# Hybrid attention and SSM encoder block: all gate products ahead of the last SSM output, the forget gate behind it, and z's work pinned behind the SSM's outputs

## The chip, the cores and the metric

The kernel runs on one core of a Trainium2 chip. The metric is the time of one execution on the device in microseconds (us), the median of several runs. TensorE is written PE, VectorE DVE, ScalarE ACT, GpSimd POOL and SyncE SP, as the profile does; PEld is PE's loading of stationary operands.

## The reference

One layer (`DEPTH = 1`) over 16 meta tokens and 1024 frames (L = 1040 positions), width 1024, all in float32:

```python
h = concatenate([meta, x])
xn = rmsnorm(h, norm_mix_g)
q, k, v, f_logit, u, gates = split(xn @ w_in)          # 512, 512, 512, 8, 512, 2048 columns
cum_f = cumsum(log_sigmoid(f_logit + b_forget))
y_a = softmax(q.k/8 + cum_f[t] - cum_f[s], s <= t) @ v @ w_attn_out    # 8 heads of 64
z = gelu(s5(u))                                        # diagonal complex SSM, 32 groups of 16 channels
zg = z @ w_glu
y_s = zg[:, :1024] * sigmoid(zg[:, 1024:])
g = sigmoid(gates)
h = h + (g[:, :1024] * y_a + g[:, 1024:] * y_s) @ w_o
xn = rmsnorm(h, norm_ffn_g)
hid = causal_conv3(xn @ w_up)                          # 5632 columns, val and gate
h = h + (silu(gate) * val) @ w_down
out = rmsnorm(h, norm_final_g)[16:]
```

## The kernel before

Features lie on partitions and positions along the free axis: the normed input is kept as `xhi` and `xlo`, its rounded part and the rest, for all L positions. A float32 product is made as three products of rounded parts (`dense_steps`, L170 to L172: high by high, high by low, low by high), eight slices of 128 input features each, so one block of outputs takes 24 products.

The stages of the part that matters here stand in this order in the program:

1. `u` is projected and written to DRAM. `ssm` (L1522) then works in four quarters of eight groups. For each quarter, `ssm_in` and `ssm_out` make tables, and `ssm_chain` is a generator of three parts: inputs (matmuls, copies on ACT), the scan over chunks of 8 positions (rotations on DVE by `TT`, which records each instruction in `log`; two scans, L1831 and L1832; the states `St`), and the outputs: 16 pairs of small products into PSUM (L1851, L1853), copies on ACT to `Y` (L1854), a GELU activation on ACT (L1855), and a store of `Y` to `y_d` in DRAM, issued by POOL (L1856).
2. `stage_gates` is a generator over the second eight gate chunks (chunk 8 to 15, the SSM branch's gates). Each chunk has 72 products in three blocks, so there are 576. A block ends with a sigmoid on ACT (L500) and a store issued by POOL (L501). `advance(q)` runs this generator up to `BEHIND[q]` products, so gate products fill PE while the SSM's other engines work.
3. `forget` (L522) makes the forget gate's logits in three blocks of 16 products (L526, L527), adds the halves (ACT L528, DVE L529), and forms the log sigmoid and its cumulative sum: DVE, ACT's Exp and Ln (L532, L533), DVE's scan, POOL's scaling (L536), a store to `f_d`. The attention reads `f_d` at 354 us.
4. `load_z` (L611) reads `y_d` back as four tiles `zt` with 32 small DMAs, issued by SP and, for the last quarter, half of them by POOL (L618). `split_z` makes z's high copy on ACT (L623) and the rest on DVE. The GLU's products are seven instead of eight (`seven`, a Strassen form), so sums and differences of z's quadrants are made: for each k of two, DVE L636, POOL L637, DVE L638 and L639, then a copy on ACT (L643) and a subtraction on DVE for each of four forms. k = 0 needs quarters 0 and 2 of the SSM, k = 1 quarters 1 and 3.
5. `project_qk(0, qk)` (L574): queries, then keys, of the first pair of heads, 72 products each in blocks of 272, 384 and 384 positions. Their weights come by `wchunk` with `act=True`: POOL issues the load, ACT casts to the high part (L154) and writes the negated copy (L143), and POOL issues a DMA that adds the weights to it in memory, which gives the low part (L144).
6. `glu` for eight chunks: weight forms (POOL L663, ACT L657, DVE or POOL L137), then `seven` (L232 to L234), then `gate`.

Weight tiles `raw`, `whi` and `wlo` have two buffers each, taken in turn by gate chunk 14, gate chunk 15, the queries, the keys, and then by the GLU's weight forms. The PSUM banks of the gate, forget, query and key blocks are three of tag `mm` and one of tag `po`, the latter taken by every fourth block.

What each engine does first is decided when the program is built: a planner lays the instructions out on a simulated time line, by program order and by when their inputs are ready there, and each engine then takes its own in the order that comes out. `after(a, b)` sets an edge without a semaphore: instruction `a` comes behind `b` in the order of their engine. DMAs issued by an engine stand in that engine's order too.

Of the kernel before, what the change touches and what calls it, by code (L numbers as in the profile page):

```python
# [13 lines left out]
AF = mybir.ActivationFunctionType  # L14
ALU = mybir.AluOpType
# [43 lines left out]
def block_kernel(ctx, tc, x, meta, xbt, x0t, g1t, w_q, w_k, w_v, w_f, w_u, w_g, b_f, w_ao, lam_d, bw_d, cw_d,  # L59
                 d_sk, l_dt, w_glu, w_o, g2, w_up, cwt_d, w_dn, gf, out, dbg=None, upto=99):  # L60
# [4 lines left out]
    V, S, GP, PE, SY = nc.vector, nc.scalar, nc.gpsimd, nc.tensor, nc.sync  # L65
# [34 lines left out]
    ident = cp.tile([P, P], F, name="ident")  # L100
# [7 lines left out]
    u_d = dp.tile([SW // P, P, P // GC, NCH], F, name="u_d")  # L108
# [27 lines left out]
    def split_lo(eng, out_, src, hi):  # L136
        return eng.tensor_tensor(out_, src, hi.bitcast(F), ALU.subtract)  # L137
# [39 lines left out]
    def run(gen):  # L177
        for _ in gen:
            pass
# [124 lines left out]
    g1T = n1.tile([P, KD], F, name="g1T")  # L304
    S.dma_start(g1T, g1t)
    GP.dma_start(xm, meta)
    ssm_log, ssm_loads, ssm_steps = ssm(tc, after, sp, sio, st_ps, ident, u_d, y_d, lam_d, bw_d, cw_d, d_sk, l_dt)
    queue = []

    def load(dst, src):  # L310
# [199 lines left out]
        for i in range(KD, 2 * KD):  # L510
            yield from gate_chunk(i, gp_, False)

    BEHIND = (288, 360, 480, 540, 552)
    gates = stage_gates()
    n_gate = [0]

    def advance(q):
        while n_gate[0] < BEHIND[q]:
            next(gates)
            n_gate[0] += 1  # L520

    def forget():  # L522
        for t, n in BLK:
            ps = mm_ps()
            for i in range(KD):
                PE.matmul(ps[:64, :n], wf[:, i, :], xhi[:, i, t:t + n], start=(i == 0), stop=False)  # L526
                PE.matmul(ps[:64, :n], wf[:, i, :], xlo[:, i, t:t + n], start=False, stop=(i == KD - 1))  # L527
            S.copy(fx[:, t:t + n], ps[32:32 + H, :n])  # L528
            V.scalar_tensor_tensor(out=fl_[:, t:t + n], in0=ps[:H, :n], scalar=bf, in1=fx[:, t:t + n],  # L529
                                   op0=ALU.add, op1=ALU.add)  # L530
        V.scalar_tensor_tensor(out=fx, in0=fl_, scalar=-1.0, in1=fl_, op0=ALU.mult, op1=ALU.max)
        S.activation(fx, fx, AF.Exp, scale=-1.0)  # L532
        S.activation(fx, fx, AF.Ln, bias=one[:H])  # L533
        V.scalar_tensor_tensor(out=fx, in0=fl_, scalar=0.0, in1=fx, op0=ALU.min, op1=ALU.subtract)
        V.tensor_tensor_scan(fl_, one[:H].broadcast_to([H, L]), fx, 0.0, ALU.mult, ALU.add)
        GP.tensor_scalar(fx, fl_, -8.0, 0.0, ALU.mult, ALU.add)  # L536
        GP.dma_start(f_d, fx)
        if "f_d" in dbg:
            SY.dma_start(dbg["f_d"], fx)
# [8 lines left out]
    for q in range(4):  # L548
# [6 lines left out]
            begin(q + 2)  # L555
        if q == 1:
            next(ssm_steps)
    advance(4)
    fl_ = sio.tile([P, L], F, tag="sy", name="fl_", bufs=3)[:H]
    fx = sx.tile([P, 1152], F, tag="Gm", name="fx", bufs=1)[:H, :L]  # L560
    forget()
    st_x.close()
    run(gates)
    st_g.close()
    st_s.close()

# [32 lines left out]
    TH = L // 2  # L599
# [11 lines left out]
    def load_z():  # L611
        zts = []
        for m in range(4):
            tag = "gl" if m % 2 else "ms"
            zt = gz[tag].tile([P, CH, NCH], F, tag=tag, name="zt", bufs=2)
            ym = y_d[m].rearrange("(j c) g n -> g c j n", c=GC)
            for g in range(GQ):
                (GP if m == 3 and g % 2 else SY).dma_start(zt[GC * g:GC * g + GC], ym[g])  # L618
            zts.append(zt)
        def split_z(m):  # L620
            w_ = NC2 if m < 2 else NCH
            zh, zl = (fold(t_[:, m % 2, :CH * w_]) for t_ in zs[m // 2])
            S.copy(zh, zts[m][:, :, :w_])  # L623
            split_lo(V, zl, zts[m][:, :, :w_], zh)

        split_z(0)
        split_z(1)

        def part(r, h_, k):
            return zts[2 * r + k][:, :, NC2 * h_:NC2 * h_ + NC2]  # L630

        T4 = zblock(0, 1)
        for k in range(2):
            fa, fb = (gz["cg"].tile([P, L], F, tag="cg", name="zf", bufs=2) for _ in range(2))
            f1, f2, f3, f4 = (fold(f_[:, TH * q:TH * q + TH]) for f_ in (fa, fb) for q in range(2))
            V.tensor_tensor(f1, part(0, 1, k), part(0, 0, k), ALU.subtract)  # L636
            GP.tensor_tensor(f3, part(1, 1, k), part(0, 1, k), ALU.subtract)  # L637
            V.tensor_tensor(f2, part(1, 1, k), f1, ALU.subtract)  # L638
            V.tensor_tensor(f4, part(1, 0, k), f2, ALU.subtract)  # L639
            for f_, t_ in zip((fa, fa, fb, fb), (T1, T2, T3, T4)):  # L640
                q = 0 if t_ is T1 or t_ is T3 else TH
                hi, lo = t_[0][:, k], t_[1][:, k]
                S.copy(hi, f_[:, q:q + TH])  # L643
                split_lo(V, lo, f_[:, q:q + TH], hi)
            split_z(2 + k)
        return T4
# [875 lines left out]
def ssm(tc, after, sp, sio, s_ps, ident, u_d, y_d, lam_d, bw_d, cw_d, d_sk, l_dt):  # L1522
# [1 line left out]
    V, S, GP, PE, SY = nc.vector, nc.scalar, nc.gpsimd, nc.tensor, nc.sync  # L1524
    n_small = [0]

    log = []

    def TS(*a):
        log.append(V.tensor_scalar(*a))  # L1530
# [31 lines left out]
    def rest():  # L1562
# [71 lines left out]
        m = sm(W)  # L1634
# [166 lines left out]
        def chain(qt):  # L1801
# [44 lines left out]
            for q in range(0, GQ, 3):  # L1846
# [5 lines left out]
                              start=True, stop=False)  # L1852
                    PE.matmul(yo, Tm[:, q + i, :], U[:, q + i, :], start=False, stop=True)  # L1853
                S.copy(Y[:, q:q + nq].rearrange("p a n -> p (a n)"), yps[:, :NCH * nq])  # L1854
            S.activation(Y, Y, AF.Gelu_apprx_tanh)  # L1855
            GP.dma_start(y_d[qt], Y)  # L1856

        yield input_tables, output_tables, chain
        rot.append(rotation(1))
        yield  # L1860

    return log, loads, rest()


_OUTS = [((1, SEQ, D), "float32")]
# [55 lines left out]
```

## Time and profile before

| | us |
|---|---|
| median of 3 runs (lowest, highest) | 1466.59 (1466.46, 1469.03) |
| the profiled execution | 1469.97 |
| its span | 1467.7 |

| engine | busy us | share of the span |
|---|---|---|
| PE | 1430.3 | 97% |
| PEld | 1350.7 | 92% |
| DVE | 1074.6 | 73% |
| POOL | 760.7 | 52% |
| ACT | 723.1 | 49% |

How to read the lines shown below. A line of a timeline has the start in us from the beginning of the span, the duration in us, the engine, the line of the kernel, the operation, its output and inputs by the program's names, the count (x2 where two neighbours were merged), and in square brackets the engine's idle time just before and what ended it. A line of the waits has who waited for whom, the total in us, the times, and the longest. A line of the stretches has the window, its length, the busy time and the number of instructions of PE, PEld, DVE, ACT and POOL, the granted clock of PE (1.00 is full), the busy share of the DMA engines and what they moved in GB/s. L137 is a helper, the subtraction that leaves the low part; the tile's name says which one it is. PE's matmuls overlap, so the spacing of their starts, not their duration, is what one costs.

### The profile page before, as it was taken

The numbers are of one execution on the slowest core, as the hardware profiler recorded it, in microseconds if no ns is written. First come the engines' busy times: TensorE is split into PE (matmuls) and PEld (weight loads), VectorE is DVE, ScalarE is ACT, GpSimd is POOL, SyncE is SP. The second block draws the span as 40 slices with busy tenths as digits, with TensorE's granted clock in tenths as the row PEclk, the third lists the DMA queues.
The fourth block names the chain that finished last, engine by engine and source line by source line (L and its number), as shares of the span: only waits on it lengthen the run. The fifth ranks groups of instructions, "written<-read, shape, count | busy, mean of one in ns | idle before, by whom it ended". The sixth has DMA issues, their size and how long they took to land. (4 is left out here: it accounts for less than half of the span.)

```text
span 1467.7 us, 26536 instructions
## 1 busy us (share of the span) xinstructions
PE 1430.3 (97%) x9646; PEld 1350.7 (92%) x9646; DVE 1074.6 (73%) x2198; ACT 723.1 (49%) x1419; POOL 760.7 (52%) x888
## 2 busy tenths in 40 slices
PE   8999979999999999999999999999999999998997
PEld 8999979988999999999879999999999999776886
DVE  7999868852657676646469977788887667688685
ACT  7646575522646565542646444444444435652433
POOL 1542137740555556515861335555554327889766
PEclk9999989999999999999999999999999999999999
DMA  8676634440126432156963245667753214866413
GB/s 281 177 185 161 151 80 127 149 142 30 37 90 171 137 68 79 44 207 237 268 152 136 81 123 163 170 171 186 181 137 109 87 66 151 308 202 164 144 36 115
DMA packets 89653, 209.31 MB, mean 143 GB/s; under 512 B 14442, under 2 KB 22266, under 8 KB 89140
## 3 DMA queue, kind: packets, MB, share of 16 engines
q1 hardware_dynamic: 70068, 162.55, 33.6%
q0 software_dynamic: 17728, 41.41, 14.7%
q10 hardware_dynamic: 1728, 3.68, 0.7%
q8 instruction: 76, 1.25, 0.4%
q14 instruction: 53, 0.43, 0.1%
HBM read 168.52 MB, written 69.35 MB: 162 GB/s over the span
## 5 line engine op out<-in xcount | busy, mean ns | idle before, releaser
L172 PE MATMUL mm<-xhi,wlo 128*128 128x342 f32 (+2 forms) x488 | 159.4, 327 | 7.4 <-DMA wlo<-in_w_k_dram 7.4
L170 PE MATMUL mm<-xhi,whi 128*128 128x342 f32 (+2 forms) x488 | 160.1, 328 | 1.3 <-DVE q L137 1.0
L171 PE MATMUL mm<-xlo,whi 128*128 128x342 f32 (+2 forms) x488 | 158.6, 325 | 0.0
L1156 POOL TENSOR_TENSOR ov<-ov,og 128x1024 f32<-128x1024 f32 x21 | 51.1, 2434 | 122.7 <-ACT og L1155 118.8
L137 DVE TENSOR_TENSOR sw<-sf,sw 128x512 fp32r<-128x512 f32 x72 | 67.0, 930 | 49.1 <-ACT sw L1147 49.1
L172 PEld LDWEIGHTS mm<-xhi,wlo 128*128 128x128 f32 x488 | 92.9, 190 | 8.0 <-DMA wlo<-in_w_k_dram 7.6
L1147 ACT CAST sw<-sf 128x512 fp32r<-128x512 f32 x72 | 44.9, 624 | 108.6 <-POOL sf L1273 66.6
L170 PEld LDWEIGHTS mm<-xhi,whi 128*128 128x128 f32 x488 | 93.0, 191 | 2.4 <-PE sp L791 0.8
L171 PEld LDWEIGHTS mm<-xlo,whi 128*128 128x128 f32 x488 | 92.9, 190 | 0.4 <-issue 0.2
L840 ACT CAST th<-tp 128x256 fp32r<-128x256 f32 (+3 forms) x120 | 56.1, 472 | 61.4 <-PE tp L833 29.1
L1273 POOL TENSOR_TENSOR sf<-raw,sf 128x512 f32<-128x512 f32 x36 | 61.2, 1699 | 44.4 <-DVE sw L137 43.3
L137 DVE TENSOR_TENSOR tl<-tp,th 128x256 fp32r<-128x256 f32 (+3 forms) x120 | 65.1, 547 | 25.4 <-ACT th L840 24.0
L1273 POOL TENSOR_TENSOR sf<-raw 128x512 f32<-128x512 f32 x36 | 47.5, 1320 | 68.6 <-DMA raw<-in_w_up_dram 35.1
L234 PE MATMUL mm<-xhi,sw 128*128 128x258 f32 (+1 forms) x288 | 81.0, 281 | 0.0
L232 PE MATMUL mm<-xhi,sw 128*128 128x258 f32 (+1 forms) x288 | 80.8, 281 | 0.0
L233 PE MATMUL mm<-xlo,sw 128*128 128x258 f32 (+1 forms) x288 | 80.7, 280 | 0.0
L805 POOL TENSOR_SCALAR pt<-pt,nm 128x144 f32<-128x144 f32 (+4 forms) x72 | 52.2, 738 | 51.7 <-DVE nm L804 50.7
L1325 DVE SCALAR_TENSOR_TENSOR ov<-hv,cwt,ov 128x1024 f32<-128x1024 f32 x36 | 71.2, 1977 | 0.1
L1147 ACT CAST sw<-raw 128x512 fp32r<-128x512 f32 x70 | 43.1, 621 | 54.8 <-PE sp L234 26.2
L803 ACT ACTIVATE pt<-pt,nm 128x144 f32<-128x144 f32 (+4 forms) x72 | 52.9, 736 | 26.8 <-DVE nm L802 26.3
L796 DVE CUSTOM_DVE_ANT_0 pt<-sp,fb 128x328 f32<-128x328 f32 (+8 forms) x112 | 46.4, 429 | 20.1 <-PE sp L791 11.5
L137 DVE TENSOR_TENSOR sw<-raw,sw 128x512 fp32r<-128x512 f32 x70 | 54.7, 784 | 5.4 <-ACT sw L1147 4.9
(719 smaller groups left out, 5715.7 us busy)
## 6 DMA issues: line engine op xcount, KB each, us to landing
raw<-in_w_up_dram SPq DMA_DIRECT2D x44, 512.0 KB, 3.7
t_d<-in_w_dn_dram POOLq DMA_DIRECT2D x44, 256.0 KB, 6.9
ar<-a_d SPq DMA_DIRECT2D x44, 256.0 KB, 5.6
wr<-t_d SPq DMA_DIRECT2D x44, 256.0 KB, 2.8
a_d<-ov SPq DMA_DIRECT2D x21, 512.0 KB, 2.6
wr<-in_w_dn_dram SPq DMA_DIRECT2D x33, 256.0 KB, 4.2
t_d<-in_w_dn_dram SPq DMA_DIRECT2D x22, 256.0 KB, 4.5
t_d<-t_d SPq DMA_DIRECT2D x22, 256.0 KB, 4.5
```

What stands on the lines that cost most here:

```text
L137: return eng.tensor_tensor(out_, src, hi.bitcast(F), ALU.subtract)
L170: yield PE.matmul(ps, whi[:, i, :], ahi[:, i], start=(i == 0), stop=False)
L171: yield PE.matmul(ps, whi[:, i, :], alo[:, i], start=False, stop=False)
L172: yield PE.matmul(ps, wlo[:, i, :], ahi[:, i], start=False, stop=(i == k - 1))
L232: PE.matmul(ps, a[0][:, i], bh, start=(i == 0 and not joins), stop=False, skip_group_check=True)
L233: PE.matmul(ps, a[0][:, i], bl, start=False, stop=False, skip_group_check=True)
L234: PE.matmul(ps, a[1][:, i], bh, start=False, stop=(i == kh - 1), skip_group_check=True)
L803: S.activation(pt[:n, :kc], pt[:n, :kc], AF.Exp, bias=nm[:n, 1:2], scale=0.125, accum_out=nm[:n, 2:3])
L840: S.copy(th[:kn, z:tw], tp[:kn, z:tw])
L1147: S.copy(hi, src)
L1273: sums.append(GP.tensor_tensor(f_, a, b, op))
L1325: V.scalar_tensor_tensor(out=o, in0=h_[:, j:SEQ + j], scalar=cwc(j, m), in1=o, op0=ALU.mult, op1=ALU.add)
```

## The change

- `ssm` also returns `outs`, which holds for each quarter the GELU activation (`outs[0]`, `[2]`, `[4]`, `[6]`) and the issue of its store (`outs[1]`, `[3]`, `[5]`, `[7]`).
- `BEHIND` becomes (288, 360, 480, 576): all gate products are called for ahead of the outputs of quarter 3. `run(gates)`, which finishes the generator, stands ahead of `forget()` and no longer behind it, and `advance(4)` goes.
- z's copies on ACT (L623) are set behind the activation of quarter 2, `outs[4]`; the copies of the forms (L643) behind that of quarter 3, `outs[6]`.
- z's subtractions on DVE in `split_z` and the form at L636 are set behind the last SSM instruction of DVE, `ssm_log[-1]`; POOL's form at L637 behind the issue of quarter 3's store, `outs[7]`.

```diff
-    BEHIND = (288, 360, 480, 540, 552)
+    BEHIND = (288, 360, 480, 576)
...
-    advance(4)
     fl_ = sio.tile([P, L], F, tag="sy", name="fl_", bufs=3)[:H]
     fx = sx.tile([P, 1152], F, tag="Gm", name="fx", bufs=1)[:H, :L]
+    run(gates)
     forget()
     st_x.close()
-    run(gates)
...
-            S.copy(zh, zts[m][:, :, :w_])
-            split_lo(V, zl, zts[m][:, :, :w_], zh)
+            after(S.copy(zh, zts[m][:, :, :w_]), ssm_outs[4])
+            after(split_lo(V, zl, zts[m][:, :, :w_], zh), ssm_log[-1])
...
-            V.tensor_tensor(f1, part(0, 1, k), part(0, 0, k), ALU.subtract)
-            GP.tensor_tensor(f3, part(1, 1, k), part(0, 1, k), ALU.subtract)
+            after(V.tensor_tensor(f1, part(0, 1, k), part(0, 0, k), ALU.subtract), ssm_log[-1])
+            after(GP.tensor_tensor(f3, part(1, 1, k), part(0, 1, k), ALU.subtract), ssm_outs[7])
...
-                S.copy(hi, f_[:, q:q + TH])
+                after(S.copy(hi, f_[:, q:q + TH]), ssm_outs[6])
...
-            S.activation(Y, Y, AF.Gelu_apprx_tanh)
-            GP.dma_start(y_d[qt], Y)
+            outs.append(S.activation(Y, Y, AF.Gelu_apprx_tanh))
+            outs.append(GP.dma_start(y_d[qt], Y))
```

More of the change, by code (lines that the diff above doesn't have):

```diff
@@ L306, in block_kernel @@
     GP.dma_start(xm, meta)
[L307 removed]
+    ssm_log, ssm_outs, ssm_loads, ssm_steps = ssm(tc, after, sp, sio, st_ps, ident, u_d, y_d, lam_d, bw_d, cw_d, d_sk, l_dt)
     queue = []
@@ L1860, in rest @@
         yield
-    return log, loads, rest()
+    return log, outs, loads, rest()
 _OUTS = [((1, SEQ, D), "float32")]
```

2 lines of the change are left out of this document (1 added, 1 removed).

## The prediction

> **What bounds the kernel now**
>
> I read the head of the page first, then PE's list of waits, then the timelines of the engines around the end of the SSM.
>
> ```profile
> span 1467.7 us, 26536 instructions
> PE 1430.3 (97%) x9646; PEld 1350.7 (92%) x9646; DVE 1074.6 (73%) x2198; ACT 723.1 (49%) x1419; POOL 760.7 (52%) x888
> PE mm L172 <- DMA wlo<-in_w_k_dram: 7.4, 1, 7.4
> PE tp L1851 <- DVE St L1533: 1.7, 1, 1.7
> PE mm L170 <- DVE fl__2308 L529: 0.3, 1, 0.3
> ```
>
> TensorE is the bound: 37.4 us of the span are not PE work. The change adds no product and removes none, so it can only move PE's waits. The three waits shown all lie between the SSM's last outputs and the GLU, where the change is; the longest single wait of the whole list is the first, for the low part of the key weights. PE's timeline around them:
>
> ```profile
> 164.94 0.38 PE L1851 MATMUL sp<-St,Gm 128*128 128x130 f32 x2
> ...
> 168.43 0.41 PE L170 MATMUL mm<-xhi,whi 128*128 128x342 f32 x1
> ...
> 174.18 0.29 PE L526 MATMUL po<-xhi,wf 128*64 128x272 f32 x1
> ...
> 178.57 0.46 PE L1851 MATMUL tp<-St,Gm 128*128 128x130 f32 x2 [1.72 <-DVE St L1533]
> ...
> 182.37 0.42 PE L527 MATMUL mm<-xlo,wf 128*64 128x384 f32 x1
> ...
> 187.48 0.32 PE L170 MATMUL mm<-xhi,whi 128*128 128x342 f32 x1
> ...
> 191.22 0.29 PE L170 MATMUL po<-xhi,whi 128*128 128x272 f32 x1
> ...
> 203.18 0.29 PE L170 MATMUL mm<-xhi,whi 128*128 128x272 f32 x1
> ...
> 211.00 0.59 PE L172 MATMUL mm<-xhi,wlo 128*128 128x272 f32 x1 [7.41 <-DMA wlo<-in_w_k_dram]
> 211.39 0.43 PE L170 MATMUL mm<-xhi,whi 128*128 128x272 f32 x1
> ...
> 216.15 0.44 PE L170 MATMUL po<-xhi,whi 128*128 128x384 f32 x1
> ...
> 224.73 0.28 PE L232 MATMUL mm<-zh,ops 128*128 128x260 f32 x1
> ```
>
> In order: outputs of SSM quarter 2 (164.94 to 168.43); 36 products of gate chunk 15 (to 174.18); 19 of the forget gate's 48; a wait for the last states; outputs of quarter 3 (178.57 to 182.37); the other 29 forget products; the last 24 products of gate chunk 15 (187.48 to 191.22); queries; keys, which stop within their first three products for 7.4 us; GLU at 224.73. After the stop the products are slow: 21 of them in 211.39 to 216.15, 0.227 us each. The 24 of the query block from 191.22 have the same shape and end at about 194.2, 0.125 us each. The stretches show why:
>
> ```profile
> 203.20:211.40 8.20, 0.79 (x5) 0.57 (x4) 7.21 (x7) 4.58 (x8) 6.02 (x3) 0.68 0.56 108
> 211.40:216.20 4.80, 4.80 (x23) 4.80 (x23) 4.74 (x5) 4.54 (x5) 2.69 (x4) 0.50 0.30 97
> 174.90:224.70 49.80, 40.38 (x244) 38.31 (x243) 33.94 (x40) 32.84 (x49) 16.90 (x17) 0.90 0.41 103
> ```
>
> (Columns: stretch, length, busy PE, PEld, DVE, ACT, POOL, granted clock, DMA share, GB/s.) The granted clock is 0.50 in the 4.8 us behind the stop. So the stop costs its 7.4 us and then 21 x 0.102 = 2.1 us.
>
> Why were the key weights late? ScalarE and POOL:
>
> ```profile
> 168.10 1.27 ACT L623 CAST zh<-zt 128x520 fp32r<-128x520 f32 x1 [2.63 <-DMA zt<-y_d]
> ...
> 186.43 0.63 ACT L643 CAST z2h<-zf 128x520 fp32r<-128x520 f32 x1 [5.30 <-DVE zf L638]
> ...
> 192.42 1.07 ACT L1855 ACTIVATE Y<-Y 128x1040 f32<-128x1040 f32 x1
> ...
> 198.76 1.04 ACT L154 CAST whi<-raw 128x1024 fp32r<-128x1024 f32 x1
> 199.82 1.28 ACT L500 ACT_TABLE_LOAD   x1
> ...
> 203.95 1.04 ACT L143 ACTIVATE wlo<-whi 128x1024 fp32r<-128x1024 f32 x1
> 205.29 0.92 POOL L144 DMA_DIRECT2D wlo<-in_w_k_dram  x1 [2.85 <-ACT wlo L143]
> 197.07 2.14 POOL L618 DMA_DIRECT2D zt<-y_d  x4 [2.73 <-DMA y_d<-Y]
> ```
>
> The cast of the key weights needs the second buffer of the weight tiles; gate chunk 15 holds it until its last product, at 191.2, because 24 of its products stand behind the forget gate. ScalarE then reaches the cast at 198.76, and cast, negated copy and adding DMA bring the low part at 211.0: 12.2 us from the start of the cast. ScalarE also shows z's copies standing ahead of the SSM's own: one waits 2.63 us at 168.10, just when quarter 2's outputs are done, another 5.30 us up to 186.43, though quarter 3's were done at 182.4, and the last activation comes only at 192.42.
>
> **The change part by part**
>
> *All 576 gate products ahead of the last outputs.* 60 gate products now follow quarter 2's outputs, at (174.18 - 168.43) / 36 = 0.160 us: PE comes to quarter 3's outputs at 168.43 + 9.6 = 178.0. No product is added. The last block's sigmoid and its store on POOL come forward with it; its table load at 199.82, which now parts the key weights' cast from its copy, should go.
>
> *z's DVE work behind the last state.* DVE's rows:
>
> ```profile
> 166.23 1.23 DVE L1831 TENSOR_TENSOR_SCAN wr<-dt,ta 128x520 f32<-128x520 f32 x1
> 168.11 1.22 DVE L636 TENSOR_TENSOR zf<-zt 128x520 f32<-128x520 f32 x1 [0.65 <-DMA zt<-y_d]
> ...
> 170.53 1.27 DVE L1832 TENSOR_TENSOR_SCAN ta<-dt,wi 128x520 f32<-128x520 f32 x1
> ...
> 176.60 1.10 DVE L137 TENSOR_TENSOR zl<-zt,zh 128x520 fp32r<-128x520 f32 x1 [0.98 <-ACT zh L623]
> 177.74 1.42 DVE L1533 TENSOR_TENSOR St<-ta,wr 64x516 f32<-64x516 f32 x2
> ```
>
> The scan at 170.53 could follow the one that ends at 167.46: 3.1 us won; the z split at 176.60, with its wait, holds the last states another 2.0. The states then end at about 179.2 - 5.1 = 174.1. PE comes at 178.0, so its 1.72 us wait goes, under cover of 3.9 us of gate products. Quarter 3's outputs took 3.80 us behind the wait and quarter 2's 3.49: 0.3 us more.
>
> *Forget gate behind the outputs.* Its 48 products cost the same there. Its results are read first at the attention, far off, but its three PSUM banks are taken again by the last two query blocks and the first key block, and copies on ScalarE and adds on DVE must clear them. Today this costs the 0.3 us of the third wait; I take 0 to 0.3 and count 0.3 as won.
>
> *The key weights.* Chunk 15 ends at 178.0, 13.2 us earlier. In the new order the keys begin at 203.18 - 1.72 - 0.3 - 0.3 = 200.9, so the cast must start by about 201.1 - 12.2 = 188.9. It has 10.9 us for that, and ScalarE, which waits for PE's outputs from 178 to 181.5 anyway, has nothing of z to do until their activation, as the pins forbid it. I take no wait: 7.4 + 2.1 us won.
>
> *z's ScalarE and POOL work behind the last activation and its store.* Quarter 3's outputs end at 178.0 + 3.5 = 181.5; a table load like the one at 199.82 (1.28) and the activation (1.07) bring 183.9, and I take 184.3 with the last copy ahead of them, against 193.5. Its store, SP's last z loads and POOL's four follow 9.2 us earlier with it; SP's loads for quarter 2 start some 1.3 us earlier, the length of the copy at 168.10. POOL's difference form for k = 0, below, ran at 185.16 when its data had come, so the pin to the store's issue at 184.3 costs nothing.
>
> *The sum.* 1.72 + 0.3 + 0.3 + 7.4 + 2.1 = 11.8 us; the GLU could begin at 212.9. What may then be late is z and the GLU's weight forms. DVE had 33.9 us of work from 174.9 to 224.7; less 1.4 for the last states and plus the form at 168.11 and one split like that at 176.60, both moved in (2.3), it is 34.8, to be done in 174.1 to 212.9, 38.8 us, of which some 5 are idle while quarter 2's z still loads (4.77 now, first row below). That is some 1 us too much, though splits of the keys' low parts in it are not needed by then. ScalarE has 32.8 less a 1.28 load in the same stretch. I bound the new wait ahead of the GLU by 0 (it fits) and 3 us (DVE's overrun and one misplaced wait, such as the 2.63 above, partly beside each other), and take the middle, 1.5, being near neither.
>
> So 11.8 - 1.5 = 10.3 us. The profiled execution took 1469.97 us, its span 1467.7 and 2.3 around it; it becomes 1459.7. The median of the unprofiled runs is 1466.59, 3.4 lower: 1456.3. Behind the GLU PE stays the bound, so the gain lasts to the end.
>
> **The rivals**
>
> *The hand-over to the GLU binds (gain 3 to 8).* z's work that used to fill DVE's and ScalarE's gaps from 168 to 182 is packed behind the outputs, with forget's chain and the query copies. For it: these rows, two-input DVE operations beside POOL's z form.
>
> ```profile
> 185.13 1.21 DVE L638 TENSOR_TENSOR zf<-zt,zf 128x520 f32<-128x520 f32 x1 [4.77 <-DMA zt<-y_d]
> 185.16 2.35 POOL L637 TENSOR_TENSOR zf<-zt 128x520 f32<-128x520 f32 x1 [5.45 <-DMA zt<-y_d]
> 186.37 2.23 DVE L639 TENSOR_TENSOR zf<-zt,zf 128x520 f32<-128x520 f32 x1
> 209.59 1.17 DVE L639 TENSOR_TENSOR zf<-zt,zf 128x520 f32<-128x520 f32 x1
> ```
>
> The same form takes 2.23 us while POOL's form runs (to 187.5) and 1.17 without it. Packed tighter, both forms and four splits so lengthened add some 6 x 1.06 = 6.4 us to a DVE that has none to spare: 11.8 - 6.4 = 5.4 us gain, 1461.2. Against it: POOL is busy 16.9 of 49.8 us there, so not all coincide. [...] The same loss comes if forget's bank copies stand behind a z copy that waits. If the 6.4 us fall in one piece, the 2.1 us of slow products come on top, as behind the 7.4, and the gain is 3.3: 1463.3; behind 1.72 us only 0.3 came. [...]
>
> *The stop stays (no change).* The planner may leave the cast near 198.76; the keys' low part then lands at 211.0 whatever comes before: 1466.6. For it: z's copies rank ahead of the projection in program order. Against: ScalarE is free when the buffer falls free.
>
> *Slower: the cast falls behind z's last copies.* The rows for it (the first is the z loads' own):
>
> ```profile
> DMA to landing us min/median/max: 2.2/3.6/7.3
> 207.58 1.06 DVE L638 TENSOR_TENSOR zf<-zt,zf 128x520 f32<-128x520 f32 x1
> 215.57 0.64 ACT L643 CAST zh<-zf 128x520 fp32r<-128x520 f32 x1
> ```
>
> POOL's last z load is issued by 199.2 now, 9.2 us earlier then, and lands 3.6 us later: 193.6. The work on k = 1 takes 207.6 to 216.2, 8.6 us: 202.2. A cast there brings the low part at 214.4, 3.4 us after today's: 1470.0. It decides from any cast later than 198.8. For it: ScalarE takes its instructions in one order, and 186.43 shows a copy placed ahead of work that was ready. Against: the buffer is free 16 us before z's last data.
>
> **How the numbers follow**
>
> Forecast (gain 8 to 12.5) 0.66; hand-over 0.14; stop stays 0.07; slower 0.13. The measurement can tell 0.2%, 2.9 us. Faster by more than that: 0.66 + 0.14 = 0.80; within: 0.07; slower: 0.13. The likeliest gives 1456.3. The range leaves out the last two cases: from 11.8 and a little for run spread (1454.0) to the hand-over's worst, in one piece, with as little for spread (1463.6).
>
> **What would show it**
>
> PE's list without the key-weight wait and without the wait for the last states; granted clock 1.00 from 200 to 220; chunk 15's last product near 178, the key cast before 189, the last activation of the SSM near 183 to 185, the first GLU product at 213 to 215. A wait at the GLU's first products for DVE means the first rival; a wait at the first L172 of the keys the second or third. It is wrong altogether if the order elsewhere changes, seen as new PE waits behind 320.

## The result and the profile after

| | before | after |
|---|---|---|
| median of 20 runs each | 1468.24 us | 1464.02 us |
| lowest, highest | 1466.05, 1469.84 | 1461.39, 1469.32 |
| ratio, 95% interval | | 0.9975 [0.9967, 0.9983] |

The change gains some 3.7 us (0.25%, the ratio on 1468.24); 10.3 were predicted. The forecast was a median of 1456.3 us, in a range of 1454.0 to 1463.6. The measured one lies 7.7 us above the forecast, and 1.65 of these are the level of the kernel before: 1468.24 here, 1466.59 when the forecast was made. The page's head:

```profile
span 1466.9 us, 26536 instructions
PE 1430.5 (98%) x9646; PEld 1351.0 (92%) x9646; DVE 1078.1 (73%) x2198; ACT 722.5 (49%) x1418; POOL 760.8 (52%) x888
```

The profiled execution after took 1469.32, the highest of its runs; 2.4 us of that lie in a wait at the very end of the kernel (`tp L1441 <- DVE hs L1451`, 5.1 us here, 2.7 before and in most of the profiles below), far from the change. Lines behind L563 have one less than before. PE's list of waits, the lines that are new or have grown (the second was 1.0 us in two before):

```profile
PE mm L232 <- ACT k L590: 3.5, 1, 3.5
PE mm L170 <- DVE q L137: 3.0, 3, 2.0
PE mm L232 <- DVE kl L137: 1.1, 1, 1.1
```

The key weights' 7.4, the states' 1.7 and the forget bank's 0.3 are gone. In their place stand three waits at the hand-over from the projection to the GLU, in PE's timeline:

```profile
209.03 0.41 PE L170 MATMUL mm<-xhi,whi 128*128 128x384 f32 x1 [1.98 <-DVE q L137]
...
217.00 0.36 PE L232 MATMUL mm<-zh,ops 128*128 128x260 f32 x1 [3.54 <-ACT k L590]
...
219.05 0.56 PE L232 MATMUL mm<-zh,ops 128*128 128x260 f32 x1 [1.08 <-DVE kl L137]
```

1.98 + 3.54 + 1.08 = 6.6 us. The GLU starts at 217.00 instead of 224.73, 7.7 earlier; its last products on `zh` show only 3.6 of it (one row of PE's products on `zh`, before and then after; the last number is the start of the last of them):

```profile
L234 PE MATMUL sp<-zh,ops x32: 277/284/286, 234.4 to 304.5; 128*128 128x260 f32 x32
```

```profile
L234 PE MATMUL sp<-zh,ops x32: 278/282/286, 230.7 to 300.9; 128*128 128x260 f32 x32
```

So some 4 us are lost inside the GLU: the wait of 1.08, and slow products behind the waits, as the stretches show (granted clock in the third column from the right):

```profile
210.00:220.00 10.00, 5.38 (x30) 4.91 (x29) 8.83 (x13) 9.03 (x17) 2.25 (x4) 0.91 0.19 57
220.00:230.00 10.00, 10.00 (x67) 10.00 (x66) 6.22 (x15) 6.76 (x18) 6.47 (x10) 0.75 0.19 58
```

Which queue was late? The engines in order of time, ScalarE, VectorE, then POOL:

```profile
177.52 1.05 ACT L154 CAST whi<-raw 128x1024 fp32r<-128x1024 f32 x1
...
181.50 1.05 ACT L143 ACTIVATE wlo<-whi 128x1024 fp32r<-128x1024 f32 x1
...
184.90 1.08 ACT L1854 ACTIVATE Y<-Y 128x1040 f32<-128x1040 f32 x1
...
208.70 4.43 ACT L622 CAST zh<-zt 128x1040 fp32r<-128x1040 f32 x2 [5.54 <-POOL fx L536]
```

```profile
184.76 1.32 DVE L637 TENSOR_TENSOR zf<-zt,zf 128x520 f32<-128x520 f32 x1 [6.94 <-DMA raw<-in_w_glu_dram]
...
197.88 1.30 DVE L637 TENSOR_TENSOR zf<-zt,zf 128x520 f32<-128x520 f32 x1 [3.00 <-DMA zt<-y_d]
...
202.47 1.23 DVE L534 SCALAR_TENSOR_TENSOR fx<-fl__2336,fx 8x1040 f32<-8x1040 f32 x1
...
204.85 2.31 DVE L535 TENSOR_TENSOR_SCAN fl__2336<-one,fx 8x1040 f32<-8x1040 f32 x1
...
207.76 1.12 DVE L137 TENSOR_TENSOR q<-mm,q 64x384 fp32r<-64x384 f32 x2
210.98 4.39 DVE L137 TENSOR_TENSOR zl<-zt,zh 128x1040 fp32r<-128x1040 f32 x2 [2.09 <-ACT zh L622]
...
218.01 0.89 DVE L137 TENSOR_TENSOR kl<-mm,k 64x272 fp32r<-64x272 f32 x2
```

```profile
182.85 0.91 POOL L144 DMA_DIRECT2D wlo<-in_w_k_dram  x1 [0.41 <-ACT wlo L143]
...
207.33 1.34 POOL L536 TENSOR_SCALAR fx<-fl__2336 8x1040 f32<-8x1040 f32 x1 [6.94 <-DVE fl__2336 L535]
```

The key weights are cast at 177.52 and their low part is asked for at 182.85: that part came as predicted. VectorE stands still twice for z's loads, 6.94 us for quarter 2's (the profile names a weight's DMA there, but the form L637 reads z) and 3.00 us for the last quarter's. Then the forget gate's chain (Exp, Ln, L534, the scan, POOL's scaling) is spread over the hand-over. ScalarE stands 5.54 us still ahead of z's second pair of copies, since that pair's memory is where the forget gate's sum `fl_` lay and POOL reads it until 208.7 (`fl_u` below shows it). VectorE's split of the second query block, which frees a bank for PE, stands behind L534 and the scan. The key copies stand behind z's copies.

### The profile page after: what moved, and what is told of

Its sections match the earlier page's. It is cut to its first block, busy times and chain, and to the rows that moved or that the text cites. A ratio compares the mean times of both kernels' runs of the same rounds, so it can differ in the third digit from the quotient of the medians.

```text
span 1466.9 us, 26536 instructions
## 1 busy us (share of the span) xinstructions
PE 1430.5 (98%) x9646; PEld 1351.0 (92%) x9646; DVE 1078.1 (73%) x2198; ACT 722.5 (49%) x1418; POOL 760.8 (52%) x888
## 5 line engine op out<-in xcount | busy, mean ns | idle before, releaser
L170 PE MATMUL mm<-xhi,whi 128*128 128x342 f32 (+2 forms) x480 | 156.6, 326 | 3.0 <-DVE q L137 3.0
L172 PE MATMUL mm<-xhi,wlo 128*128 128x342 f32 (+2 forms) x480 | 155.5, 325 | 0.0
L171 PE MATMUL mm<-xlo,whi 128*128 128x342 f32 (+2 forms) x480 | 155.0, 323 | 0.0
```

The source lines that it names most:

```text
L170: yield PE.matmul(ps, whi[:, i, :], ahi[:, i], start=(i == 0), stop=False)
L171: yield PE.matmul(ps, whi[:, i, :], alo[:, i], start=False, stop=False)
L172: yield PE.matmul(ps, wlo[:, i, :], ahi[:, i], start=False, stop=(i == k - 1))
```

## The experiments

Three theories of what holds PE at the hand-over were tested one after the other. A: the memory of the forget gate's sum, for which z's copies wait. C: the place of the forget gate's chain in the three engines' orders, whatever its work. B: the amount of work there, VectorE's above all, whatever its order.

Each kernel was timed in five rounds against the kernel before on the same chip. All start from the change, but for `b_fl_u`. The median of the kernel before was between 1466.98 and 1470.00 us in the several rounds, so a difference of 0.1% between two rows says little.

| run | what differs from the change | ratio to before [95%] |
|---|---|---|
| p_gates | without z's pins | 0.9985 [0.9976, 0.9994] |
| p_pins | z's pins alone | 1.0002 [0.9993, 1.0010] |
| fl_u | forget's sum in memory of its own | 0.9959 [0.9945, 0.9972] |
| fl_gm | the same in another slot; queues reordered | 1.0004 [0.9993, 1.0014] |
| b_fl_u | before, with fl_u's edit | 1.0000 [0.9991, 1.0010] |
| f_mid | forget between the last gate product and the outputs | 0.9951 [0.9937, 0.9965] |
| f_early | forget ahead of the last 96 gate products | 0.9964 [0.9948, 0.9980] |
| nochain | without forget's L531 to L535 | 0.9928 [0.9914, 0.9942] |
| tailpin | fl_u; L534 and the scan behind the second query split | 0.9969 [0.9956, 0.9982] |
| nozl_u | fl_u without z's two long remainders | 0.9945 [0.9928, 0.9963] |
| nozl_mid | f_mid without them | 0.9949 [0.9932, 0.9967] |
| bare | without L531 to L535 and without them | 0.9906 [0.9888, 0.9924] |
| f_mid_z | f_mid, the two behind T's forms | 0.9967 [0.9955, 0.9980] |
| f_mid_k0 | f_mid, the two behind the first key split | 0.9974 [0.9963, 0.9984] |
| f_mid_k1 | f_mid, the two behind the second key split | 0.9973 [0.9961, 0.9985] |
| f_pin | f_mid, Exp behind the last activation | 0.9959 [0.9944, 0.9973] |
| f_pin_u | f_pin with fl_u's edit | 0.9963 [0.9951, 0.9976] |
| f_pin_zv | f_pin, the two behind the first six weight remainders | 0.9964 [0.9949, 0.9978] |

**The two halves.** `p_gates` has the change without the lines on z; `p_pins` the lines on z alone.

> Only the gate and forget part of the change, without the pins on z. Theory A: the stop at the key weights goes (9.5 us), z's copies stand ahead of the SSM's outputs again, the wait for fl_ stays but comes behind all query copies, so it costs less than in the changed kernel: ratio 0.993 to 0.996. Theory B (the pins' packing is what costs): the whole gain of 11 us, ratio 0.992 or lower, with VectorE's waits gone.

> Only the pins on z, with the gate and forget order of before. Both theories: the states come some 5 us earlier and PE's 1.7 us wait for them goes, the stop at the key weights stays unless the ScalarE reaches the cast earlier. Theory A: ratio 0.997 to 0.999. Theory B: the packing costs here too, ratio 1.000 to 1.003.

```profile
PE mm L172 <- DMA wlo<-in_w_k_dram: 8.5, 1, 8.5
```

Alone, the pins win the states' wait and leave the 8.5 us stop: nothing, as theory B said and not A. Alone, the gates win the stop but the last activation stays at 189.50, and the gain is 0.15%: less than either theory said. PE's list there has 7.4 us of waits in five places, 3.0 and 2.0 of them for a key and a query split, so the hand-over costs without the pins too. Both together give 0.25%; the intervals of the gates alone and of both overlap.

**The memory.** `fl_u` changes the slot, and no engine's order:

```diff
-    fl_ = sio.tile([P, L], F, tag="sy", name="fl_", bufs=3)[:H]
+    fl_ = sio.tile([P, L], F, tag="U", name="fl_", bufs=2)[:H]
```

`fl_gm` takes `sp.tile([P, 1152], F, tag="Gm", name="fl_", bufs=2)` instead, and `b_fl_u` is the first edit in the kernel before.

> The changed kernel with the forget gate's sums (fl_) in the U slot of the SSM's pool, which z's second pair of tiles does not cover; every engine's order is that of the changed kernel. Theory A (z's copy of quarter 2 on ScalarE waits until POOL has read fl_, because it writes the same memory, and the query and key copies stand behind it): that wait of 5.5 us goes, with it PE's 1.98 + 3.54 + 1.08 us and the slow products behind them, about 3 us; 9 to 10 us under the changed kernel, ratio to before 0.991. Theory B (VectorE and ScalarE have too much work at the hand-over, the wait is only where it shows): at most 2 us, ratio 0.996 to 0.9975.

> The changed kernel with fl_ in the Gm slot of the SSM's first pool instead. The planner then puts z's copies of quarters 2 and 3 ahead of the query copies on ScalarE; orders of PE, POOL and SyncE stay. Theory A: again 9 to 10 us under the changed kernel, ratio 0.991, within 2 us of the U slot. Theory B: ratio 0.996 to 0.9975, or worse than the U slot, since more of z is packed ahead of the query copies.

> The kernel before with the forget gate's sum in the tag U's memory in place of sy's, nothing else: a control for the 2.4 us that the same edit gave on top of the change. Where the forget chain stands ahead of the last outputs, z's second copy waited 0.3 us for it only. Theory C': no difference, ratio 0.9985 to 1.0015. If the memory's place itself is worth something apart from that wait: 0.9975 to 0.999.

With its memory free, z's copies start at 201.87 and the ratio falls from 0.9975 to 0.9959, some 2.4 us (the intervals overlap, so the size is not sharp). In the kernel before, the same edit gives nothing, so the new place in memory is worth nothing by itself, and what it gives on top of the change is put down to that wait. Theory A, that this was all of the loss, expected about four times as much, and falls. `fl_gm` can't be read as a memory test: the planner also moved z's copies and splits ahead of the queries', and PE waits 9.5 us for a query split. It shows what order alone can cost, 4.2 us against the change. In `fl_u` the 1.98 us wait for the query split is still there, and something new appears. VectorE, POOL, ScalarE:

```profile
207.31 4.18 DVE L137 TENSOR_TENSOR zl<-zt,zh 128x1040 fp32r<-128x1040 f32 x2
211.41 0.41 DVE L137 TENSOR_TENSOR ops<-raw,ops 128x256 fp32r<-128x256 f32 x1
```

```profile
207.92 4.49 POOL L662 TENSOR_TENSOR sf<-raw 128x256 f32<-128x256 f32 x1
```

```profile
212.45 0.41 ACT L656 CAST ops<-sf 128x256 fp32r<-128x256 f32 x1 [4.33 <-POOL sf L662]
```

A weight sum that takes POOL 0.76 us elsewhere takes 4.49, while VectorE runs z's two long remainders (`zl`, 128x1040), and ScalarE's weight copy, with the key copies behind it, waits 4.33 for it.

**The chain's place, and the chain itself.** In `f_mid` and `f_early` the two tile lines and `forget()` stand in the loop over quarters, under `if q == 3:`, behind or ahead of `advance(q)`. `tailpin` is `fl_u` with two VectorE instructions moved (z's last copies on ScalarE fall behind with them); `nochain` leaves five out.

```diff
 # tailpin
+                    cut = split_lo(V, t_["q1"][:64, s_], p1, t_["q1"][64:, s_])
+                    if pr == 0 and t == BLK[1][0]:
+                        after(tail[0], cut)          # tail[0] is L534
 # nochain
-        V.scalar_tensor_tensor(out=fx, in0=fl_, scalar=-1.0, in1=fl_, op0=ALU.mult, op1=ALU.max)
...
-        V.tensor_tensor_scan(fl_, one[:H].broadcast_to([H, L]), fx, 0.0, ALU.mult, ALU.add)
```

> The change with forget's products set between chunk 15's last product and quarter 3's outputs, so that its chain of vector and scalar instructions runs while TensorE is still on the outputs; the gate chunks and z's pins stay as in the change, and no instruction is left out. Theory C (the forget gate's chain, standing in the three queues behind the last outputs, holds the query splits and POOL's weight sums, and what it costs is its place, not its work): the waits at the hand-over (1.98, 3.54 and 1.08 us in the change) shrink to under 2 us together, the GLU's first product comes at 207 to 211 instead of 217.0, and the ratio to the kernel before is 0.991 to 0.994 (1456 to 1459 us); up to 3 us of that may be lost again where Exp and Ln with their table loads stand ahead of the last outputs' activation. Theory B (the hand-over has too much work for VectorE and ScalarE: z's forms, query and key copies, whatever the place of the forget gate): the waits stay at 5 us or more, the GLU starts at 215 or later and the ratio is that of the change, 0.9965 to 0.9985.

> The change with forget's products one step earlier still, right behind quarter 2's outputs and ahead of the last 96 gate products, so that the whole chain runs beside the gate products. ScalarE then has to change between the tables of Sigmoid, Exp and Ln among the gate activations, three more loads of 1.28 us. Theory C: as for the kernel with forget between the products and the outputs, or better by the chain's 8 us being out of the way of the outputs as well: waits at the hand-over under 2 us, GLU from 206 to 210, ratio 0.990 to 0.994. Theory B: waits of 5 us or more stay, ratio 0.9965 to 0.9985. A third way: the forget logits' bank is read late in ScalarE's queue and TensorE waits for it 1 to 4 us ahead of the gate products; then the ratio is 0.993 to 0.997 with a wait named for L529.

> The change with the five instructions of the forget chain between its logits and POOL's scaling left out (L531 to L535: absolute value, Exp, Ln, subtraction, scan); it leaves out the log of the sigmoid and the running sum. VectorE loses some 6.5 us of work and ScalarE some 5 us with its table loads, all of it behind the last outputs. Theory C: the waits at the hand-over shrink to under 1.5 us together, the GLU starts at 206 to 210, ratio 0.990 to 0.993. Theory B: less work but the rest still too much: waits of 4 us or more, GLU at 213 or later, ratio 0.995 to 0.998.

> The change with forget's sum in memory of its own (as in the earlier kernel at ratio 0.9959) and the chain's last two VectorE instructions (L534 and the scan) placed behind the query split of the second block; all else in its order but for z's last copies, which fall behind. Theory C for VectorE alone: the wait of 1.98 us for that split goes (under 0.5), and since POOL's scaling and so its weight sums now come some 5 us later, the key copies behind the sums on ScalarE come later too: a wait of 3 us or more for a key copy, and a ratio of 0.996 to 0.998, no better than memory alone. If the weight sums don't matter, 0.993 to 0.995. Theory B: the wait for the split stays at 1.5 us or more.

Without the chain the gain is 0.72%, 10.6 us: as much as was predicted for the whole change. With the chain only moved, 0.49% and 0.36%, between theories C and B. The waits did not shrink as C said; they changed their names: 5.9 us in two places in `f_mid`, 6.8 in three in `f_early`. `f_mid`, PE and VectorE:

```profile
216.28 0.56 PE L232 MATMUL mm<-zh,ops 128*128 128x260 f32 x1 [5.22 <-DVE kl L137]
```

```profile
211.30 2.04 DVE L137 TENSOR_TENSOR zl<-zt,zh 128x1040 fp32r<-128x1040 f32 x1
213.25 1.63 DVE L639 TENSOR_TENSOR zf<-zt,zf 128x520 f32<-128x520 f32 x1
...
215.25 0.89 DVE L137 TENSOR_TENSOR kl<-mm,k 64x272 fp32r<-64x272 f32 x2
```

Here the first key split stands behind a long remainder and one of z's forms, and PE waits 5.22 us for its bank. In `tailpin` the wait for the query split went, as expected, PE waited for the key split instead, and the ratio of 0.9969 was in the range that theory C gave for VectorE alone:

```profile
217.03 0.56 PE L232 MATMUL mm<-zh,ops 128*128 128x260 f32 x1 [4.28 <-DVE kl L137]
```

**z's long remainders.** In `nozl_u`, `nozl_mid` and `bare` they are replaced, in place:

```diff
-            after(split_lo(V, zl, zts[m][:, :, :w_], zh), ssm_log[-1])
+            if m < 2:
+                after(split_lo(V, zl, zts[m][:, :, :w_], zh), ssm_log[-1])
+            else:
+                after(V.memset(zs[1][1][:, m % 2].bitcast(F), 0.0), ssm_log[-1])
```

> The change with the forget gate's sum in memory of its own (ratio 0.9959), and z's two long remainders (zl of its second pair, 128x1040, 4.4 us on VectorE) replaced by two fills with zero at the same place in VectorE's queue; it leaves out the low part of half of z. The forget chain stays where the change puts it. Theory B (VectorE's work at the hand-over, and POOL held by it): POOL's weight sum that took 4.49 us falls to under 1.3 us, the waits behind the first query split go, ratio 0.992 to 0.994. Theory C (the forget chain's place in the queues): the first query wait of 1.98 us stays, and little else changes: ratio 0.995 to 0.9965.

> The same replacement in the kernel with forget between the last gate product and quarter 3's outputs (ratio 0.9951). Theory B: the wait of 5.22 us for the key split falls to under 2 us and nothing of its size takes its place; ratio 0.991 to 0.993. Theory C: with the chain out of the way already, the rest is small: ratio 0.9935 to 0.996.

> Both left out: the forget chain's five instructions (ratio 0.9928 alone) and z's two long remainders; what the GLU's start costs when neither stands in a queue. If the two causes are one (too much for VectorE there), there is little left for the second: 0.991 to 0.993. If they are two separate ones, 0.988 to 0.991. The gain that the prediction reckoned with, without its 1.5 us for a new wait, is 11.8 us, a ratio of 0.992.

In `nozl_u` POOL's sum is short again:

```profile
208.21 0.76 POOL L665 TENSOR_TENSOR sf<-raw 128x256 f32<-128x256 f32 x1
```

The gain rises from 0.41% to 0.55% (the intervals overlap), less than theory B said, as the query wait of 1.98 us behind the chain stays. `nozl_mid` went against theory B: nothing gained over `f_mid`, and 3.54 us of wait for the key split remain, now behind z's forms without the remainders. With both the chain and the remainders away, PE has no wait of a microsecond between the last outputs and the end of the GLU's first products. `bare`'s stretches:

```profile
200.00:210.00 10.00, 9.93 (x61) 9.74 (x60) 9.75 (x19) 8.26 (x20) 2.54 (x5) 1.00 0.36 108
210.00:220.00 10.00, 10.00 (x84) 10.00 (x83) 7.01 (x15) 6.58 (x18) 6.56 (x9) 1.00 0.16 54
```

VectorE is full even so (9.75 of 10 us). Its ratio of 0.9906 is 13.8 us (the interval is 11.2 to 16.4): the 11.8 us that the prediction counted ahead of its new wait were there. Between `nochain` and `bare` the remainders are worth 0.22%, 3 us, with intervals that overlap; between `nozl_u` and `bare` the chain is worth 0.39%, 6 us, with intervals apart.

**The same work in other orders.** `f_mid_z`, `f_mid_k0` and `f_mid_k1` place `zl` of the second pair with `after(z_, ...)` behind T's last remainder, the first or the second key split; hardly anything else in the queues moves. `f_pin` adds `after(fexp, ssm_outs[6])` to `f_mid`, `fexp` being Exp.

> The kernel with forget between the last gate product and quarter 3's outputs, and on VectorE alone the two remainders of z's second pair (zl, 2.39 and 2.04 us) placed behind the last remainder of T's forms; no other instruction changes its place in any queue. Theory C', as it stands after the runs before (nothing is short of time in total; one engine's queue holds what TensorE needs next behind what it needs later, here the first key split behind the two zl): that split comes some 4.4 us earlier, TensorE's wait of 5.22 us for it falls to under 1.5 us, no wait of more than 1.5 us takes its place at the third product of the GLU (which is the first to read zl, 12 us after the first), and the ratio to before falls from 0.9951 to 0.991 to 0.993. Theory B (VectorE has too much to do there in whatever order): the wait moves to zl, to z's forms or to a bank behind the next key split, at 3 us or more, and the ratio stays at 0.994 to 0.996.

> The same with the two remainders directly behind the key split of the first block, and so ahead of T2's and T3's remainders, which the GLU's second product reads. Theory C': the wait of 5.22 us for the key split goes as above, but T2's remainder comes at about 218 as in the kernel without the placement while TensorE now wants it at 213 to 215: a wait of 2 to 4 us for z2l (or for the bank behind it) takes its place, and the ratio is 0.993 to 0.995, between the two. Theory B: as above, 0.994 to 0.996, and no difference between this kernel and the one with the remainders behind T's forms.

> The kernel with forget between the products and the outputs, and z's two long remainders behind the key split of the second block (one step later than behind T's forms, ratio 0.9967); nothing left out. Theory of the held POOL: POOL's weight remainder starts before the long ones and takes 0.7 to 1.5 us instead of 4.53, the wait of 3.9 us for it falls to under 1.5 us, and at most 2 us come back as a wait for zl at the GLU's third product; ratio 0.993 to 0.995. Theory of load: the wait is only renamed again (zl or a bank, 3 us or more), ratio 0.9955 to 0.9975.

> Forget's products and logits between the last gate product and quarter 3's outputs as before, and its Exp placed behind the last activation of the outputs on ScalarE; all instructions of the reference are there. If what was left of the loss there was z's late last quarter: last activation from 184 to 187 instead of 193.92, the scan over by 200 to 204, waits of under 3 us together between the queries and the GLU, ratio 0.992 to 0.9945. If VectorE's load decides: the long remainders stand ahead of the key split and of the first weights' remainders, a wait of 3 us or more for one of them, ratio 0.9945 to 0.9965.

> The same with the forget gate's sum in the tag U's memory; the order of all queues is the same. If z's second copies still wait there for POOL's scaling (as in the change, 5.54 us), this one is faster by 1 to 3 us; if the chain is over before z's copies come up, both are the same within 0.1%.

> The kernel with forget early and its Exp behind the last activation (ratio 0.9959), with all seven weight remainders of the first GLU chunk on VectorE (POOL's two among them) and z's two long remainders behind the sixth of them, so that POOL's weight sums meet none of the long ones and the first two key splits stand ahead of them. If an order was all that was missing: POOL's sums take 0.7 to 1.5 us instead of 6.46, TensorE waits under 3 us in all, most of it for zl at the third product, ratio 0.992 to 0.9945. If VectorE's work decides: 4 us or more of waits, under whatever names (the key split's bank, zl), ratio 0.9945 to 0.997.

In `f_mid_z` the wait for the key split fell to 2.31, and PE waited 3.9 us for a weight remainder of POOL instead, which VectorE's long ones hold; the ratio of 0.9967 is worse than either theory said. PE's waits, POOL, VectorE:

```profile
PE tp L234 <- POOL ops L137: 3.9, 1, 3.9
```

```profile
214.95 4.53 POOL L137 TENSOR_TENSOR ops<-sf,ops 128x256 fp32r<-128x256 f32 x1 [1.85 <-ACT ops L662]
```

```profile
214.80 4.09 DVE L137 TENSOR_TENSOR zl<-zt,zh 128x1040 fp32r<-128x1040 f32 x2
218.92 1.12 DVE L137 TENSOR_TENSOR kl<-po,k 64x384 fp32r<-64x384 f32 x2
```

In `f_mid_k0` it was T2's remainder, as expected, but the ratio of 0.9974 is again outside both ranges; in `f_mid_k1` POOL's remainder was early and short (0.73 us at 215.23), as expected, and the second key split and `zl` itself late, and the ratio of 0.9973 is the one of the theory of load:

```profile
216.81 0.59 PE L233 MATMUL sp<-z2l,ops 128*128 128x260 f32 x1 [3.54 <-DVE z2l L137]
```

```profile
213.01 0.36 PE L232 MATMUL mm<-zh,ops 128*128 128x260 f32 x1 [2.28 <-DVE kl L137]
...
221.21 0.58 PE L233 MATMUL mm<-zl,ops 128*128 128x260 f32 x1 [1.84 <-DVE zl L137]
```

`f_pin` brought z's last quarter 5 to 7 us earlier (last activation at 188.47 instead of 193.92, where 184 to 187 was expected; the form that is L638 in `f_mid` at 202.91 instead of 209.84), and gained nothing by it: POOL's sum was held 6.46 us, the key split came at 214.18. `f_pin_u` is the same within its interval. The reason is not that the chain is over by then: in `f_pin` z's copies start at 200.54 and POOL's scaling runs at 201.82, but the copies no longer wait for it. `f_pin_zv` takes away both the hold of POOL and the long wait for the key split, and pays in small waits, 4.0 us together, of which the three longest follow, and a slow clock (0.67 in 220 to 230); its ratio is in the range given for VectorE's work:

```profile
212.05 0.36 PE L232 MATMUL mm<-zh,ops 128*128 128x260 f32 x1 [1.18 <-DVE kl L137]
...
218.22 0.39 PE L232 MATMUL mm<-zh,ops 128*128 128x260 f32 x1 [1.47 <-ACT c L241]
...
220.39 0.58 PE L233 MATMUL mm<-zl,ops 128*128 128x260 f32 x1 [0.94 <-DVE zl L137]
```

Ten kernels with all the work, and the forget chain's memory or place mended, lie between 0.9951 and 0.9974 (`fl_gm`, with its queues reordered, at 1.0004); the two that leave the chain out lie at 0.9928 and 0.9906. The best with all the work, by the ratio, are `f_mid`, then `fl_u` and `f_pin`, all faster than before. The intervals of `fl_u` and `f_pin` overlap the change's. That of `f_mid` ends just short of it (0.9965 against 0.9967), but it is the best of ten, in the rounds in which the kernel before was at its highest median, so a gain over the change is not shown.

## Why the prediction was wrong

**Ahead of the hand-over the steps of the sum held, but z came late.** Quarter 3's outputs began at 176.9 (178.0 predicted) without a wait; the key cast at 177.52, before 188.9; the low part's DMA at 182.85. The states' and the forget bank's waits, the stop and the half clock behind it went (the granted clock was 1.00 from 206 to 218). `bare` shows what these are worth when nothing takes their place: 13.8 us by its ratio, with an interval that holds the 11.8 of the sum. The last activation was over at 185.98 (184.3 predicted), 7.5 us earlier than before and not 9.2; POOL's z loads started at 191.48, 5.6 earlier; and the first VectorE form on the last quarter at 197.88, where the prediction's own figures bring the data at 193.6.

**The step that failed is the last term of the sum, the new wait ahead of the GLU: 1.5 us, bounded by 3.** It measured 6.6 us of waits and some 3 of slow products. Three things in it were wrong.

*The cover that the stop gave to other engines was left out.* The reckoning gave VectorE 34.8 us of work in 174.1 to 212.9, some 5 us of idle time, and so 1 us too much. In the change it was busy 25.2 us in that stretch and idle 13.6, the 6.94 and 3.00 us for z's loads among them; by the reckoning's own figure 9.6 us of work were left over at 212.9. For z's last quarter comes back only at 197.9, and what depends on it, with the forget chain's tail and the splits that free PE's banks, has to go through VectorE behind that, where it is idle for 2.1 us (ahead of 210.98) in the 20 us from 197.88 to 218. In the kernel before, the stop covered such work: VectorE was busy 7.21 of the 8.20 us from 203.20 to 211.40.

*The chain of the forget gate was priced by its banks alone.* "Its results are read first at the attention, far off" is true and was the wrong question: its instructions on three engines take their places in queues, and its memory is wanted by the next tile. Leaving its five instructions out is worth 0.47%, 6.9 us (0.9975 to 0.9928, intervals apart). The profile of the kernel before held a row that says so, and I passed over it; its 0.26 us became 5.54 when the chain moved:

```profile
211.72 4.07 ACT L623 CAST zh<-zt 128x1040 fp32r<-128x1040 f32 x2 [0.26 <-POOL fx L536]
```

*The price of POOL beside VectorE.* The first rival had the right place, and its gain of 3 to 8 is where the result lies; it had 0.14. Its mechanism is only a part: it let the loss come from lengthened VectorE forms (1.17 to 2.23), and in the change two forms were lengthened, L635 at 189.50 to 1.94 and L638 at 199.22 to 2.30, some 1.9 us together. That its 6.4 us came close to the 6.6 of the waits is chance. In four of the other kernels the other side shows: a weight sum or remainder of POOL, 0.76 us in `nozl_u`, took 4.49 us in `fl_u`, 4.53 in `f_mid_z`, 6.46 in `f_pin` and 7.44 in `nochain`. In the change itself POOL's first sums (0.76 and 0.74 at 209.53 and 210.36) started before the long remainders (210.98) and were not held.

The other half of it, that the slow products come on top where the loss falls in one piece (2.1 us behind the 7.4, only 0.3 behind the 1.72), is wrong too: in the change they came behind waits of 3.54 and 1.08 us, and in `fl_u` behind one of 1.98; the numbers are in the last section.

**What is shown and what is not.** Shown: that the memory wait was there and goes with another slot (by `fl_u`; its 2.4 us are at the edge of what the intervals tell); that the chain is worth some 6 to 7 us (by `nochain` and `bare`); that with chain and remainders left out nothing of the loss remains (by `bare`); that POOL is held by the remainders (by `nozl_u`: 0.76 us, where `fl_u` has 4.49). That it is the amount of work on VectorE, and not its order, is supported by eight orders with all the work (`f_mid`, `f_early`, `tailpin`, the three that place `zl`, `f_pin` and `f_pin_zv`), none of which came near. Against it stands that leaving out the remainders alone, 4.4 us of VectorE, gave less than that theory said in `nozl_u` and nothing in `nozl_mid`. So it is not shown: an order of all three queues that does as well as `nochain` may exist, and none that I made did.

## What to carry to other kernels

A wait that is taken away was cover for other engines (VectorE was busy 7.21 of the stop's 8.20 us here): before counting it as gain, write down what each engine must finish in its order between the last input's arrival and the first product behind the wait, and set it against that interval alone, not against the whole stage. An operation whose result is needed late is still not free where it stands: each of its instructions holds a place in a queue, and its buffers hold memory that the next stage's tiles may be laid over (here the chain was worth 6.9 us by `nochain`, the wait for its memory some 2.4 by `fl_u`); the small waits in the list before a change (0.3 us here) name such places. When each new order only renames the wait, ask what could be taken out of the stretch: here leaving the chain out gave what no order gave, while leaving out z's remainders alone gave nothing clear.

## What the runs showed of the hardware

POOL's weight sums and remainders, 0.73 to 0.80 us long in `nozl_u`, which leaves VectorE's two long remainders out, were held beside those remainders, and longer than one instruction of VectorE lasted: in each of four kernels one ended 0.6 us behind the last of an unbroken run of VectorE instructions whose inputs are all in SBUF. In `nochain` it started beside a form (L633, 199.47, 1.38 us) and took 7.44 us, over the five remainders that follow:

```profile
200.21 7.44 POOL L657 TENSOR_TENSOR sf<-raw 128x256 f32<-128x256 f32 x1
```

```profile
200.73 4.53 DVE L137 TENSOR_TENSOR zl<-zt,zh 128x1040 fp32r<-128x1040 f32 x2
205.17 0.67 DVE L137 TENSOR_TENSOR z2l<-zf,z2h 128x520 fp32r<-128x520 f32 x1
205.78 0.68 DVE L137 TENSOR_TENSOR z3l<-zf,z3h 128x520 fp32r<-128x520 f32 x1
206.38 0.67 DVE L137 TENSOR_TENSOR zl<-zf,zh 128x520 fp32r<-128x520 f32 x1
207.07 1.12 DVE L137 TENSOR_TENSOR q<-mm,q 64x384 fp32r<-64x384 f32 x2
```

The run ends ahead of the split of a query block, whose first input is in PSUM (207.07), and POOL's sum 0.6 us behind the run (200.21 + 7.44 = 207.65, against 206.38 + 0.67 = 207.05). In `fl_u`, `f_mid_z` and `f_pin` it is the same (212.41 behind 211.82, 219.48 behind 218.89, 214.74 behind 214.16). It is not so without exception: in `f_pin` the sum before the held one took only 0.76 us at 207.44, beside two long remainders that took 5.07 us from 207.26. Why a remainder holds POOL, and why not in that place, no run shows.

The granted clock did not follow the length of a wait. The same wait of 1.98 us for the query split, 209.03 in the change and 207.43 in `fl_u`, left the clock alone in the one and halved it in the other. The 24 products behind it took 4.10 us from the first start to the last in the change, 5.66 in `fl_u`. The next stretches of 2 us, the change, then `fl_u` (granted clock again in the third column from the right):

```profile
210.00:212.00 2.00, 2.00 (x13) 2.00 (x12) 1.02 (x1) 2.00 (x2) 1.03 (x2) 1.00 0.13 21
```

```profile
208.00:210.00 2.00, 2.00 (x9) 2.00 (x8) 2.00 (x2) 0.12 (x1) 2.00 (x1) 0.52 0.13 17
```

Behind waits of 3.54 us it was 0.50 for 6.8 us in the change (where 1.08 us of wait followed) and for 3.4 in `nozl_mid`; behind 2.68 in `nochain`, for 3.4; behind the 1.98 in `fl_u` and in `nozl_u`, for 3.4; around and behind the 7.41 in the kernel before, for 10.2. In `f_pin_zv`, whose longest wait there was 1.47, it was 6.8; in `bare` it stayed at 1.00 from 200 to 230. So the halved stretches, worked out from the mean clock of windows as half clock against full, last once, twice or three times 3.4 us in these seven kernels, and not in proportion to the wait. What decides between them is not shown: no run here shifts a wait alone. A wait of 2 us at this place is to be priced at 2 us, or at 2 us and some 1.6 of slow products (5.66 - 4.10).
